# Storing one tile in thirteen pieces and waiting for the last stores in a section of their own

## The chip, the cores and the metric

The kernel runs on one core of one Trainium2 chip. The core has five engines that run side by side: TensorE (PE; its weight loads are shown apart as PEld), VectorE (DVE), ScalarE (ACT), GpSimd (POOL) and SyncE (SP), which here only issues DMA transfers and waits. Data moves between the chip's main memory and the on-chip memory (128 partitions) by 16 DMA engines. The metric is the device time of one execution in microseconds, as the median of several runs.

## The reference

```python
# x: (16, 512, 1024), weight: (1024, 768), bias: (768,), residual: (16, 512, 768), all float32
def reference(x, weight, bias, residual):
    return (np.matmul(x, weight) + bias + residual).astype(np.float32)
```

Seen as two dimensions, x has 8192 rows of 1024 numbers, and the output 8192 rows of 768.

## The kernel before

The 8192 rows are 64 tiles of 128 rows. Sixteen tiles (J, line 13) make one of four stretches S, and partition p holds the rows p*16 to p*16+15 of its stretch, so that a transfer of several tiles moves one long run per partition. A row of one tile in the output is 768 numbers, 3072 bytes.

For each tile, ScalarE (sometimes VectorE) casts the 128x1024 block of x to bf16 (`cast`, line 225), TensorE transposes it (`transp`, line 237), VectorE copies the transposed block out of PSUM, and TensorE multiplies it with the resident weight in sixteen matmuls (`mm_all`, line 264; each of eight weight halves, with 512 and 256 columns). GpSimd adds bias to residual (`pool_adds`, line 277), and VectorE adds the product to that (`finish`, line 291) in R, a ring of 32 tile rows that also receives the residual and is what is stored. The last tile, 63, is multiplied in two column parts of 512 and 256 (`LAST`, line 37), each added and stored by itself.

Nothing is issued as the program is written down. Every operation is recorded by `Program.add` (line 51) with what it reads and writes; `Program.emit` (line 62) then gives each engine its own list, and puts a wait on a semaphore before an operation only where no earlier wait already implies it (lines 89 to 105). A DMA gets a semaphore of its own (`landed_`, line 99), which has reached 16 when all parts of the transfer have landed.

All transfers go through SyncE, in the order of the list `ORDER` (lines 30 to 36). `pump` (line 165) takes the next entry when the recorded program has come far enough. An entry `('s', 3, 10, 11, 104)` stores, of stretch 3, the tiles from 10 to before 11 (tile 58 of all), cut at row 104: two transfers, of partitions 0 to 103 and 104 to 127 (lines 204 to 208). The stores at the end are: tiles 48 to 57 in one, tile 58 in two parts, tiles 59 and 60 in one, tile 61, tile 62, and the two column parts of tile 63 (`'c'`). SyncE waits for VectorE before each of them, so a store can be issued no earlier than the last add of its tiles, and no earlier than everything in front of it on SyncE.

Each store is given a name in `stores` (line 208), and a last operation on SyncE without an instruction of its own (line 362) depends on all of them: it only waits. `emit` leaves out those waits that others imply. The whole program stands in one section that the framework fences off (line 363): when SyncE's list is through, SyncE raises a semaphore; the other four engines, which wait for it, drain and report; SyncE collects the reports; and then all five go through the barrier that ends the program, in which GpSimd also clears the semaphores.

Of the kernel before, what the change touches and what calls it, by code (L numbers as in the profile page):

```python
# [14 lines left out]
RR = 32  # L15
# [16 lines left out]
 ('r', 0, 6, 16), ('x', 0, 14, 16), ('x', 1, 0, 6), ('r', 1, 0, 6), ('x', 1, 6, 16),  # L32
 ('r', 1, 6, 16), ('s', 0, 0, 16), ('x', 2, 0, 6), ('r', 2, 0, 6), ('x', 2, 6, 16),
 ('r', 2, 6, 16), ('s', 1, 0, 16), ('x', 3, 0, 6), ('r', 3, 0, 7), ('x', 3, 6, 16),
 ('r', 3, 7, 16), ('s', 2, 0, 16), ('s', 3, 0, 10), ('s', 3, 10, 11, 104), ('s', 3, 11, 13),
 ('s', 3, 13, 14), ('s', 3, 14, 15), ('c', 3, 15, 0), ('c', 3, 15, 1)]
LAST = [(0, 512), (512, 256)]


class Program:  # L40
# [10 lines left out]
    def add(self, eng, emit, rd=(), wr=(), dma=False):  # L51
        n, ops = len(self.ops), self.ops
        deps = {self.writer[k] for k in (*rd, *wr) if k in self.writer and (eng != "pe" or ops[self.writer[k]][0] != eng)}
        for k in wr:
            deps.update(d for d in self.readers.get(k, ()) if ops[d][0] != eng or ops[d][3])
        for k in rd:
            self.readers.setdefault(k, set()).add(n)
        for k in wr:
            self.writer[k], self.readers[k] = n, set()
        self.ops.append((eng, emit, deps - {n}, dma))  # L60

    def emit(self):
        ops, known = self.ops, {e: {} for e in self.engines}
        lane, count, snap, waits = [], {}, [], []
        for n, (eng, _, deps, dma) in enumerate(ops):
            mine = (n, 0) if dma else (eng, count.setdefault(eng, 0) + 1)
            if not dma:
                count[eng] += 1
            seen = known[eng]
            need = {}  # L70
            for d in deps:
                f, i = lane[d]
                if seen.get(f, -1) < i and i > need.get(f, (-1, 0))[0]:
                    need[f] = (i, d)
            need = {
                f: (i, d) for f, (i, d) in need.items()
                if not any(snap[d2].get(f, -1) >= i for g, (_, d2) in need.items() if g != f)
            }
            for f, (i, d) in need.items():
                for g, v in (*snap[d].items(), (f, i)):  # L80
                    if seen.get(g, -1) < v:
                        seen[g] = v
            waits.append([d for _, d in need.values()])
            lane.append(mine)
            own = dict(seen)
            own[mine[0]] = mine[1]
            snap.append(own)
        told = {d for w in waits for d in w}
        sems = {e: self.tc.alloc_semaphore(f"done_{e}") for e in self.engines if e != "sp"}
        total, mark = dict.fromkeys(self.engines, 0), {}  # L90
        for n, (eng, emit, _, dma) in enumerate(ops):
            e = self.engines[eng]
            for d in waits[n]:
                e.wait_ge(*mark[d])  # L94
            if emit is None:
                continue
            ins = emit(e)
            if dma:
                sem = self.tc.alloc_semaphore(f"landed_{n}")
                mark[n] = (sem, 16)  # L100
                ins.then_inc(sem, 16)
            elif n in told:
                total[eng] += 1
                mark[n] = (sems[eng], total[eng])
                ins.then_inc(sems[eng], 1)


@with_exitstack
def kernel(
# [8 lines left out]
    nc = tc.nc  # L118
# [33 lines left out]
    prog = Program(tc)  # L152
    op = prog.add

    def rows(a, b, cs=range(len(chunks))):
        return [("R", r % RR, c) for r in range(a, b) for c in cs]

    def dma(dst, src, rd, wr):
        op("sp", lambda e: e.dma_start(out=dst, in_=src), rd, wr, dma=True)  # L159
# [3 lines left out]
    stores = []  # L163

    def pump():
        while queue:
            kind, S, j0, j1, *cut = queue[0]
            if kind == "c":
                need = [("outc", j1)]
            elif kind in ("w", "b"):  # L170
                need = []
            elif kind == "x":
                need = [("cast", t - XR) for t in range(J * S + j0, J * S + j1) if t >= XR]
            elif kind == "r":
                need = [("store", t - RR) for t in range(J * S + j0, J * S + j1) if t >= RR]
                at = [t % RR for t in range(J * S + j0, J * S + j1)]
                if S < RR // J and any(W_ROW <= r < W_ROW + 2 * n_q for r in at):
                    need.append(("wcast", n_q - 1))
                if S < RR // J:
                    need += [("add", t) for t in range(EARLY_END) if TMP_ROW + t in at]  # L180
            else:
                need = [("out", J * S + j) for j in range(j0, j1)]
            if not all(n in done for n in need):
                return
            queue.pop(0)
            t0, nj = J * S + j0, j1 - j0
            if kind == "b":
                dma(bias_row.rearrange("(g p) n -> g p n", p=QUAD)[:, 0, :],
                    bias[None, :].to_broadcast([P // QUAD, N]), [], ["bias_row"])
                continue  # L190
            if kind == "w":
                dma(w_st[:, 2 * S + j0:2 * S + j1, :], w_d[:, S, j0:j1, :], [],
                    rows(W_ROW + 2 * S + j0, W_ROW + 2 * S + j1))
                continue
            if kind == "x":
                dma(X[:, t0 % XR:t0 % XR + nj, :], x_d[S, :, j0:j1, :], [],
                    [("X", t % XR) for t in range(t0, t0 + nj)])
            elif kind == "r":
                dma(R[:, t0 % RR:t0 % RR + nj, :], res_d[S, :, j0:j1, :], [], rows(t0, t0 + nj))
            else:  # L200
                n0, nl = (0, N) if kind == "s" else LAST[j1]
                cs = range(len(chunks)) if kind == "s" else [j1]
                j1 = j1 if kind == "s" else j0 + 1
                edges = [0, *cut, P]
                for p0, p1 in zip(edges, edges[1:]):
                    dma(out_d[S, p0:p1, j0:j1, n0:n0 + nl],
                        R[p0:p1, t0 % RR:t0 % RR + j1 - j0, n0:n0 + nl], rows(t0, t0 + j1 - j0, cs), [("out", len(stores))])
                    stores.append(("out", len(stores)))
                done.update(("store", J * S + j) for j in range(j0, j1))
            done.update((kind, J * S + j) for j in range(j0, j1))  # L210

    def mark(*what):
        done.add(what)
        pump()
# [31 lines left out]
    def times(po, lhsT, rhs, first, final, rd, wr):  # L246
        def emit(e):
            return e.add_instruction(mybir.InstMatmult(  # L248
                name=nc.get_next_instruction_name(),
                ins=[e.lower_ap(rhs), e.lower_ap(lhsT, for_matmul_weights=True)], outs=[e.lower_ap(po)],  # L250
                start_tensor_calc=first, stop_tensor_calc=final,
                tile_size=(P, P), tile_position=(0, 0), ldweights=False,
            ))
        op("pe", emit, rd, wr)
# [46 lines left out]
    def dummies(n, i):  # L301
# [10 lines left out]
        out=ident, in_=ident, compare_op=mybir.AluOpType.not_equal, fill=1.0, base=0,  # L312
        pattern=[[-1, P]], channel_multiplier=1,
    ), ["ident"], ["ident"])
    dummies(WARM, 0)

    pump()
    for kind, *a in HEAD_ORDER:
        if kind == "bias":
# [9 lines left out]
        elif kind == "wc":  # L329
            q, e, eng = a  # L330
            r = W_ROW + 2 * q + e
# [3 lines left out]
        else:  # L335
            mm_all(a[0], [a[1]])
    pump()
    for t in range(HEAD - 1):
        if ("fin", t) not in done:
# [11 lines left out]
    t = n_t - 1  # L351
    for i, (n0, nl) in enumerate(LAST):
        b = (t - 2 * i) % HEAD
# [5 lines left out]
    mark("out", t)  # L359
    pump()  # L360
    assert not queue, queue
    op("sp", None, stores)
    with tc.tile_critical():  # L363
        prog.emit()


# [28 lines left out]
```

## Time and profile before

| | us |
|---|---|
| median of 8 runs | 211.02 |
| lowest and highest of them | 210.71, 211.27 |
| the profiled execution, its own time | 211.61 |
| its span, first to last instruction | 209.83 |
| PE busy in the span | 200.3 (95%) |
| DVE, ACT, POOL busy | 105.4, 66.1, 115.1 |
| moved by DMA | 87.20 MB, mean 416 GB/s |

The page is one profiled execution. Its span leaves out 1.78 us of that execution's time. "SPq" in a view is SyncE's queue of DMA issues: a line gives the start and the duration of the issue, not of the transfer. Times in views count from the start of the span. The views leave out semaphore instructions, whose starts and durations the trace records too, as it does the start, size and duration of each packet (one row moved by one DMA engine) and the time of each landing.

### The profile page before, as it was taken

How to read it: one execution, taken by the hardware profiler on the slowest of the kernel's cores; microseconds unless marked ns; L12 is line 12 of the kernel's file. 1: busy time of each engine (PE TensorE's matmuls, PEld its weight loads, DVE VectorE, ACT ScalarE, POOL GpSimd, SP SyncE). 2: the span in 40 equal slices, each digit the busy share in tenths (PEclk: the TensorE clock that was granted, in tenths of full speed). 3: DMA queues.
4: the chain of work that ended last, by engine and by line, in shares of the span. 5: the costliest groups of instructions: out<-in, count | busy, mean ns of one | idle time of the engine just before them, and what ended most of it. 6: DMA issues, size and time to landing. Idle time of an engine off the chain costs nothing.

```text
span 209.8 us, 2462 instructions
## 1 busy us (share of the span) xinstructions
PE 200.3 (95%) x1273; PEld 80.8 (39%) x794; DVE 105.4 (50%) x141; ACT 66.1 (32%) x69; POOL 115.1 (55%) x71
## 2 busy tenths in 40 slices
PE   7899999999999999999999999999999999999990
PEld 2333433443444344334434443443344344434440
DVE  1457555445545554554455444645544554455460
ACT  2444513312730372310460083310280065230000
POOL 1100029769999805997039603999009931999000
PEclk9999999999999999999999999999999999999996
DMA  6999999999999898999999999998999999999993
GB/s 221 425 428 434 431 419 466 392 456 420 468 391 484 378 465 383 422 445 439 405 435 487 392 433 465 450 408 373 448 462 406 445 414 466 431 440 401 402 373 120
DMA packets 4924, 87.20 MB, mean 416 GB/s; under 512 B 557, under 2 KB 685, under 8 KB 1841
## 3 DMA queue, kind: packets, MB, share of 16 engines
q1 hardware_dynamic: 4913, 87.05, 97.4%
q8 instruction: 8, 0.13, 0.2%
q14 instruction: 3, 0.02, 0.0%
HBM read 61.88 MB, written 25.17 MB: 415 GB/s over the span
## 4 chain that ended last, share of the span: by engine, by line
PE 88%; DMA 7%; SPq 2%; issue 1%; ACT 0%; DVE 0%; ACTq 0%
PE psum_o L248 75%; PE pt L241 13%; DMA x_tile<-in_x_dram 7%; SPq L159 2%; ACT xb L217 0%; DVE ro L220 0%; SPq L390 0%; ACTq L94 0%; SPq L363 0%
## 5 line engine op out<-in xcount | busy, mean ns | idle before, releaser
L248 PE MATMUL psum_o<-w_sb,xt 128*128 128x256 bf16 (+1 forms) x999 | 175.3, 324 | 1.8 <-DVE xt L217 0.5
L220 POOL TENSOR_TENSOR ro<-ro,bias_sb 128x768 f32<-128x768 f32 x50 | 88.8, 1811 | 46.6 <-DMA ro<-in_residual_dram 46.6
L217 ACT CAST xb<-x_tile 128x1024 bf16<-128x1024 f32 (+1 forms) x63 | 61.3, 1022 | 117.2 <-DMA x_tile<-in_x_dram 75.7
L259 PEld LDWEIGHTS <-xt 128*128 128x128 bf16 x520 | 50.9, 98 | 102.9 <-issue 101.1
L217 DVE COPY xt<-pt 128x1024 bf16<-128x1024 bf16 x64 | 44.1, 691 | 84.4 <-PE pt L241 84.3
L220 DVE TENSOR_TENSOR ro<-psum_o,ro 128x768 f32<-128x768 f32 (+2 forms) x51 | 47.6, 934 | 5.4 <-POOL ro L220 3.3
L241 PE MATMUL pt<-ident,xb 128*128 128x128 f32 x256 | 38.3, 273 | 0.7 <-DVE xb L217 0.5
L220 POOL TENSOR_TENSOR ro<-ro 128x768 f32<-128x768 f32 x14 | 24.9, 1811 | 25.1 <-DMA ro<-in_residual_dram 24.9
L241 PEld LDWEIGHTS pt<-ident,xb 128*128 128x128 f32 x256 | 29.8, 141 | 15.7 <-issue 13.2
L220 DVE TENSOR_TENSOR ro<-psum_o,bias_sb 128x768 f32<-128x768 f32 x14 | 13.2, 948 | 0.0
L303 PE MATMUL psum_o<-warm 128*128 128x512 bf16 x18 | 6.3, 508 | 1.4 <-DVE warm_a L223 1.4
L217 DVE CAST xb<-x_tile 128x512 bf16<-128x512 f32 (+1 forms) x4 | 1.9, 492 | 6.2 <-DMA x_tile<-in_x_dram 6.2
L217 ACT CAST w_sb<-ro 128x768 bf16<-128x768 f32 x4 | 3.3, 832 | 3.8 <-DMA ro<-in_weight_dram 3.8
L217 POOL CAST w_sb<-ro 128x768 bf16<-128x768 f32 x1 | 0.8, 824 | 6.0 <-DMA ro<-in_weight_dram 6.0
L303 PEld LDWEIGHTS psum_o<-warm 128*128 128x128 bf16 x18 | 2.2, 125 | 4.5 <-issue 2.7
L217 DVE CAST w_sb<-ro 128x768 bf16<-128x768 f32 x3 | 1.7, 557 | 2.1 <-DMA ro<-in_weight_dram 2.1
L217 ACT ACT_TABLE_LOAD x1 | 1.3, 1283 | 0.9 <-SPq L363 0.9
L320 DVE STREAM_SHUFFLE bias_sb<-bias_row 128x768 f32<-128x768 f32 x1 | 1.0, 1007 | 0.0
L223 DVE MEMSET warm<- 128x256 uint32 x1 | 0.3, 272 | 1.1 <-SPq L363 1.1
L223 DVE MEMSET bias_row<- 128x768 f32 x1 | 0.7, 698 | 0.2 <-issue 0.2
L223 POOL MEMSET ident<- 128x128 f32 x1 | 0.2, 204 | 0.5 <-SPq L363 0.5
L311 POOL TENSOR_SCALAR_AFFINE_SELECT ident<-ident 128x128 f32<-128x128 f32 x1 | 0.3, 292 | 0.2 <-POOL ident L223 0.2
(7 smaller groups left out, 0.7 us busy)
## 6 DMA issues: line engine op xcount, KB each, us to landing
out_dram<-ro SPq DMA_DIRECT2D x3, 6144.0 KB, 34.1
x_tile<-in_x_dram SPq DMA_DIRECT2D x3, 5120.0 KB, 24.5
ro<-in_residual_dram SPq DMA_DIRECT2D x3, 3840.0 KB, 31.9
x_tile<-in_x_dram SPq DMA_DIRECT2D x3, 3072.0 KB, 39.5
ro<-in_residual_dram SPq DMA_DIRECT2D x3, 2304.0 KB, 18.6
x_tile<-in_x_dram SPq DMA_DIRECT2D x4, 1024.0 KB, 11.0
x_tile<-in_x_dram SPq DMA_DIRECT2D x2, 2048.0 KB, 23.5
out_dram<-ro SPq DMA_DIRECT2D x1, 3840.0 KB, 12.8
```

What stands on the lines that cost most here:

```text
L159: op("sp", lambda e: e.dma_start(out=dst, in_=src), rd, wr, dma=True)
L217: op(eng, lambda e: (e.copy if eng == "act" else e.tensor_copy)(out=dst, in_=src), rd, wr)
L220: op(eng, lambda e: e.tensor_add(out=dst, in0=a, in1=b), rd, wr)
L223: op(eng, lambda e: e.memset(dst, v), [], [wr])
L241: op("pe", lambda e, q=q: e.transpose(out=pt[:, q, :], in_=words[:, ts(q, P)], identity=ident), [("XB", t % XB_N, 2 * q // n_q), "ident"], ...
L248: return e.add_instruction(mybir.InstMatmult(name=nc.get_next_instruction_name(), ins=[e.lower_ap(rhs), e.lower_ap(lhsT, for_matmul_weight ...
L259: op("pe", lambda g: g.ldweights(lhsT), rd)
L303: op("pe", lambda e: e.matmul(PO[i][:, 0:512], lhsT=warm[:, 0:P], rhs=warm, start=True, stop=True), ["warm"], [("PO", i)])
L311: op("pool", lambda e: e.affine_select(out=ident, in_=ident, compare_op=mybir.AluOpType.not_equal, fill=1.0, base=0, pattern=[[-1, P]], ch ...
L320: op("dve", lambda e: e.stream_shuffle(out=bias_sb, in_=bias_row, mask=[0] * QUAD), ["bias_row"], ["bias"])
```

## The change

Two edits. Tile 58 is stored in thirteen transfers in place of two: partitions 0 to 47, 48 to 50, 51 to 62, then eleven, ten, nine and so on down to two partitions. And the waits for the stores are no longer an operation of the recorded program: `emit` returns the semaphores and values of all stores; SyncE waits for all but the last four of them (tiles 61 and 62 and the two parts of tile 63) at the end of the first section, and for those four in a second section in which SyncE alone takes part. The first section's exit, with all engines reporting to SyncE, so stands between the two groups of waits. These waits are written out one by one, without leaving out those that others imply: beside the thirteen pieces of tile 58, the stores of tiles 0 to 15, 16 to 31, 32 to 47, 48 to 57, and 59 with 60 are waited for in the first section.

```diff
- ('r', 3, 7, 16), ('s', 2, 0, 16), ('s', 3, 0, 10), ('s', 3, 10, 11, 104), ('s', 3, 11, 13),
+ ('r', 3, 7, 16), ('s', 2, 0, 16), ('s', 3, 0, 10), ('s', 3, 10, 11, 48, 51, 63, 74, 84, 93, 101, 108, 114, 119, 123, 126), ('s', 3, 11, 13),
  ('s', 3, 13, 14), ('s', 3, 14, 15), ('c', 3, 15, 0), ('c', 3, 15, 1)]
+OUTSIDE = 4
...
-    def emit(self):
+    def emit(self, ends):
...
-            if emit is None:
-                continue
             ins = emit(e)
...
+        return [mark[n] for n in ends]
...
                     dma(out_d[S, p0:p1, j0:j1, n0:n0 + nl],
-                        R[p0:p1, t0 % RR:t0 % RR + j1 - j0, n0:n0 + nl], rows(t0, t0 + j1 - j0, cs), [("out", len(stores))])
-                    stores.append(("out", len(stores)))
+                        R[p0:p1, t0 % RR:t0 % RR + j1 - j0, n0:n0 + nl], rows(t0, t0 + j1 - j0, cs), [])
+                    stores.append(len(prog.ops) - 1)
...
-    op("sp", None, stores)
     with tc.tile_critical():
-        prog.emit()
+        landed = prog.emit(stores)
+        for sem, value in landed[:-OUTSIDE]:
+            nc.sync.wait_ge(sem, value)
+    with tc.tile_critical(sync_engine=mybir.EngineType.SP):
+        for sem, value in reversed(landed[-OUTSIDE:]):
+            nc.sync.wait_ge(sem, value)
```

## The prediction

> **What bounds the kernel now.** I read the page's chain first, then the chain in order of time from 190 us on, to see where the work that sets the end stops being TensorE's.
>
> ```profile
> PE 88%; DMA 7%; SPq 2%; issue 1%; ACT 0%; DVE 0%; ACTq 0%
> ...
> 199.03 5.21 PE psum_o L248 x32
> 204.24 0.02 issue
> 204.27 0.42 DVE ro L220
> ```
>
> Up to 204.2 us the kernel is a TensorE kernel, and the change touches nothing there. The last add ends at 204.69. The span is 209.83, so 5.1 us come after all arithmetic: stores, their landings, and the way out of the program. Next I cut this stretch by time (columns: stretch, its length, busy time of PE, PEld, DVE, ACT, POOL, granted clock, share of the 16 DMA engines, GB/s).
>
> ```profile
> 201.00:205.00 4.00, 3.23 (x20) 1.67 (x17) 2.08 (x3) 0.00 (x0) 0.00 (x0) 1.00 0.95 377
> 205.00:206.00 1.00, 0.00 (x0) 0.00 (x0) 0.00 (x0) 0.00 (x0) 0.00 (x0) 1.00 0.85 332
> 206.00:207.00 1.00, 0.00 (x0) 0.00 (x0) 0.00 (x0) 0.00 (x0) 0.00 (x0) 0.84 0.49 175
> 207.00:208.00 1.00, 0.00 (x0) 0.00 (x0) 0.00 (x0) 0.00 (x0) 0.00 (x0) 0.50 0.05 18
> 208.00:210.00 2.00, 0.00 (x0) 0.00 (x0) 0.00 (x0) 0.00 (x0) 0.00 (x0) 0.50 0.00 0
> ```
>
> The reader is to see the row of 207 to 208: 0.05 of 16 engines is 0.8 of one engine. One DMA engine is still storing when fifteen are done. The trace's records of single packets and landings say the same: fifteen of the last store's sixteen parts land by 207.19, the sixteenth at 208.16, 0.97 us later; its data ends at 207.83, that of the others by 206.74. Then SyncE's waits go: the last landing's wait ends at 208.18, two more already fulfilled follow at 0.067 us each, and the program ends at 209.83. So 1.65 us lie behind the last landing.
>
> Third, SyncE's queue when it issues the stores of the end (start, duration; the first two are tile 58, rows 0 to 103 and 104 to 127, then tiles 59 and 60, 61, 62 and the two parts of 63).
>
> ```profile
> 191.54 0.35 SPq L159 DMA_DIRECT2D out_dram<-ro  x1
> 191.93 1.25 SPq L159 DMA_DIRECT2D out_dram<-ro  x1
> 197.61 0.35 SPq L159 DMA_DIRECT2D out_dram<-ro  x1
> 200.65 0.36 SPq L159 DMA_DIRECT2D out_dram<-ro  x1
> ...
> 204.72 0.90 SPq L159 DMA_DIRECT2D out_dram<-ro  x1
> ```
>
> Two are long: the second part of tile 58 (1.25) and the last store (0.90). The first byte of the last store moves at 206.12, 0.50 after its issue ends.
>
> [...] The trace agrees on k: the 104-row store leaves 13 engine landings and one record at 192.05, before any data; the 24-row store 12 and one early. [...] here the landing comes 0.34 us after the last packet (207.83 to 208.16), and the change leaves that alone. [...]
>
> **The change, part 1: tile 58 cut differently.** [...]
>
> Who can take rows? By the packets, the engines end the store before tile 58 (tiles 48 to 57) at 198.94, 199.13, 199.26, 199.28, 199.67, 199.89, 200.02, 200.43, 200.50, and seven between 200.66 and 200.97: a spread of 2.0 us. The records do not name an engine[...]. A 3072-byte row takes 0.121, started 0.118 apart. The late engine is one that ends at 200.86 and then needs 2.2 us for its ten rows, because eight of its packets take 0.12 to 0.43 instead of 0.121.
>
> I add up per engine: end of tiles 48 to 57, plus rows x 0.118, then eight packets each of the next five stores (0.231, 0.118, 0.118, 0.081, 0.0425 apart: 4.7 us), none before its data can start (0.5 after its issue). For the kernel before, with 1.0 of slow packets on the late engine, this gives 207.80 against 207.83 in the trace; without them 206.80. For the kernel after: 206.4 to 206.5 with no slow packets, 206.7 with half a microsecond of them and 207.2 with a whole one on an engine with eight rows. The data thus ends 0.6 to 1.4 earlier in this execution, and 0.3 to 0.4 earlier where slow packets do not occur at all (206.80 to 206.4). The last issue should also lose its 0.90: while it stands, the late engine has over thirty packets queued.
>
> **Part 2: eleven more issues.** A following issue takes 0.43 and a gap of 0.045, by the second of the two stores at 62.48 and 62.96. Thirteen from 191.54: 0.395 for the first, 12 x 0.48 = 5.76, so SyncE is free at 197.7; with one hold like that of 1.25 (0.8 more) 198.5, with a second of a microsecond 199.5. Tiles 59 and 60 are ready at 197.61, behind all this on SyncE, so their issue slips by 0 to 2 us. What is late next: their packets. Engines reach them only at about 199.6 (earliest, three rows after 199.26) to 201.5, and my sum is unmoved for an issue as late as 200; at 201 it gives 206.6, at 202 207.6. Cover gone, each further microsecond costs one. Tiles 61 and 62 are ready at 200.65 and 202.65, and nothing else is queued on SyncE; no engine waits for these rows of R.
>
> **Part 3: the landings.** Added on SyncE: waits for two old stores and eleven pieces, some ten instructions in the first section, 0.067 each when fulfilled: 0.67 after the last issue (205.1 to 205.6), so 206.3 at the latest. Then the exit of the first section, which before runs from 208.31 to 208.85 (0.54), at about 206.9, beside the last packets and landings: hidden. If cover were gone it would cost what it does today. After the last landing, before: two waits (0.13), branch to exit (0.16), drain (0.09), collecting five engines (0.21), two drains to the barrier (0.14). After: one branch, exit, drain, one NoOp, two drains; one wait (0.067) and most of the collection (0.211 to about 0.085) fall away: 0.067 + 0.126 = 0.19 saved. Bounds: 0 if the second section's own entry is late, 0.35 if its no-ops cost nothing. The final barrier and clearing (0.9) stay.
>
> **The sum.** The profiled execution took 211.61: span 209.83 and 1.78 around it. In it I expect 206.7 instead of 207.83 for data (-1.1) and -0.2 for the exit: 210.3. The median of the runs shown is 211.02, 0.6 less, so some slow packets may be of the profiled execution alone. With all of them the median goes to 209.7, with none (-0.4 - 0.2) to 210.4. I take 210.0.
>
> **The rivals.**
> 1. *Short stores are slow to issue* (slower). For it: the only two issues seen with k under 16 that follow another at once took 0.65 (bias) and 1.25 (24 rows), neither 0.43. Against it: the 104-row store also has k under 16 and took 0.35 after its wait, like 16-engine stores; two 16-engine loads were held for 1.60 and 1.34 at 95.6 and 144.1, while a 16 KB instruction fetch ran, so holds come without small k. It decides from about 0.86 per piece: then tiles 59 and 60 are issued at 202.2 and the data ends at today's 207.83. At 0.9 the end is 1.1 later than now: 211.02 + 1.1 - 0.2 = 211.9. At 1.25 they go at 207.4, data ends at 213.0, and the time is 216.
> 2. *The low engines are not the early ones.* Then 15 rows fall on an engine that ends at 200.97: +5 x 0.118 = 0.6 on such an engine, against the 1.0 of slow packets now: 210.8 to 211.4, no change.
> 3. *The cut does nothing, the section alone works*: slow packets follow whichever engine is last[...]. 211.02 - 0.2 = 210.8, inside what cannot be told. If the added waits end after the last landing, not even that: 211.0.
>
> **How the numbers follow.** The forecast has 0.60 (209.4 to 210.6), rivals 2 and 3 together 0.15, rival 1 with anything else that delays the last stores 0.25, of which half lies above 212.5. A measurement of this kernel tells from no change what exceeds about 0.2%, 0.42 us: faster is under 210.60, slower over 211.44. So 0.60 faster, 0.15 same, 0.25 slower. The range goes from 209.5 to 212.5, with under a tenth left out below and an eighth above; the forecast's own range is 209.4 to 210.6.
>
> **What would show it.** Right: the DMA share of the last stretch with data falls from many engines to none within half a microsecond, with no stretch of 0.05; the sixteen landings of the last store lie within 0.5; the thirteen issues end before 200; the last issue takes under 0.5; and the time from last landing to end is 1.45 instead of 1.65. Wrong: tiles 59 and 60 issued after 202, a DMA share well under 0.9 between 200 and 204, or again one engine behind the rest by a microsecond[...].

## The result and the profile after

The changed kernel takes 211.6 us in the median of 11 runs (211.30 to 211.78); the kernel before, run beside it, 210.89. The ratio is 1.0029, with a 95% interval of 1.0020 to 1.0039: slower by 0.6 us, which is small but clear of the noise. Faster by 1.0 had been forecast.

The chain and the chain in order of time show that TensorE's part is as it was:

```profile
PE 91%; DMA 4%; issue 1%; ACT 1%; DVE 1%; SPq 0%
...
198.96 5.21 PE psum_o L249 x32
204.17 0.02 issue
204.19 0.42 DVE ro L221
```

The difference lies after, and in SyncE's queue of issues (start, duration):

```profile
191.47 0.34 SPq L160 DMA_DIRECT2D out_dram<-ro  x1
191.85 1.10 SPq L160 DMA_DIRECT2D out_dram<-ro  x1
193.00 1.02 SPq L160 DMA_DIRECT2D out_dram<-ro  x1
...
196.54 1.21 SPq L160 DMA_DIRECT2D out_dram<-ro  x1
...
200.01 0.29 SPq L160 DMA_DIRECT2D out_dram<-ro  x1
...
201.64 0.36 SPq L160 DMA_DIRECT2D out_dram<-ro  x1
202.04 0.43 SPq L160 DMA_DIRECT2D out_dram<-ro  x1
...
204.75 1.11 SPq L160 DMA_DIRECT2D out_dram<-ro  x1
```

Of the twelve pieces that follow the first, six hold SyncE for 1.10, 1.02, 1.19, 1.21, 1.21 and 1.84, and the last six for 0.25 to 0.30. Tiles 59 and 60, finished at 197.5, are issued at 201.64 in place of 197.61. What that does to the DMA engines is seen in the stretches (length, busy time of PE, PEld, DVE, ACT, POOL, clock, DMA share, GB/s; a share near 1 means all sixteen engines busy). First the kernel before, then the changed one:

```profile
201.00:202.00 1.00, 1.00 (x7) 0.49 (x5) 0.33 (x1) 0.00 (x0) 0.00 (x0) 1.00 0.99 390
202.00:203.00 1.00, 1.00 (x7) 0.41 (x5) 0.62 (x1) 0.00 (x0) 0.00 (x0) 1.00 1.01 399
```

```profile
201.00:202.00 1.00, 1.00 (x7) 0.45 (x5) 0.41 (x1) 0.00 (x0) 0.00 (x0) 1.00 0.37 135
202.00:203.00 1.00, 1.00 (x6) 0.49 (x5) 0.55 (x1) 0.00 (x0) 0.00 (x0) 1.00 0.62 249
203.00:204.00 1.00, 1.00 (x10) 0.69 (x8) 0.61 (x1) 0.00 (x0) 0.00 (x0) 1.00 1.03 418
...
206.00:207.00 1.00, 0.00 (x0) 0.00 (x0) 0.00 (x0) 0.00 (x0) 0.00 (x0) 1.00 1.00 383
207.00:208.00 1.00, 0.00 (x0) 0.00 (x0) 0.00 (x0) 0.00 (x0) 0.00 (x0) 1.00 0.44 152
208.00:210.00 2.00, 0.00 (x0) 0.00 (x0) 0.00 (x0) 0.00 (x0) 0.00 (x0) 0.85 0.01 4
```

The shares of 0.99 and 1.01 between 201 and 203 have become 0.37 and 0.62: the engines run dry. The last packet of tile 58 ends at 202.34, and the first sixteen packets of tiles 59 and 60 start between 202.48 and 202.63. From 203 to 207 the shares are 0.94 to 1.03, and all stop together: the last store's sixteen landings lie between 207.75 and 207.91. No engine is late in this execution. That all of them had waited for the same store is a likely reason, but it isn't shown; with padding, below, the same cut has a late engine again. The last landing is 0.25 earlier than in the profiled execution before, and yet the span is no shorter, because the way out grew. From the trace's semaphore instructions and landings, in us:

```
                          last landing   to the end of the span   outside the span
before                        208.16             1.67                   1.78
changed                       207.91             2.00                   1.78
```

In the changed kernel SyncE pauses on its way out, between two of its drains at 208.34 and 208.80, which before stood 0.06 apart; the next fetch of 8 KB of instructions comes at 209.44, where the kernel before has none.

### The profile page after: what moved, and what is told of

It reads as the page before. It is cut to its first block, busy times and chain, and to the rows that moved or that the text cites. A ratio compares the mean times of both kernels' runs of the same rounds, so it can differ in the third digit from the quotient of the medians.

```text
span 209.9 us, 2488 instructions
## 1 busy us (share of the span) xinstructions
PE 199.9 (95%) x1273; PEld 80.8 (38%) x794; DVE 105.4 (50%) x141; ACT 66.1 (32%) x69; POOL 115.1 (55%) x71
## 4 chain that ended last, share of the span: by engine, by line
PE 91%; DMA 4%; issue 1%; ACT 1%; DVE 1%; SPq 0%
PE psum_o L249 78%; PE pt L242 13%; DMA x_tile<-in_x_dram 4%; ACT xb L218 1%; SPq L160 0%; DVE xt L218 0%; DVE ro L221 0%; SPq L395 0%; SPq L363 0%
```

## The experiments

**The two edits apart.** The cut alone is the kernel before with the list entry of the thirteen pieces; the section alone is the changed kernel with the old entry.

```diff
 # the cut alone
-('s', 3, 10, 11, 104)
+('s', 3, 10, 11, 48, 51, 63, 74, 84, 93, 101, 108, 114, 119, 123, 126)
 # the section alone: the reverse, in the changed kernel
```

> The kernel before with the thirteen pieces alone; the landings are waited for as before. Theory A (the short stores hold SyncE about 1.1 us each, so tiles 59 and 60 are issued at about 201.6 in place of 197.6 and the DMA engines run dry between 202 and 204; the cut carries the loss on the data side, the second section carries a loss of its own at the exit): issue of tiles 59 and 60 at 201.3 to 202, last landing near 207.9, last landing to end about 1.7, time 0.1 to 0.4 us above the kernel before, and 0.2 to 0.4 below the changed kernel. Theory B (the second section costs everything, the cut nothing): time equal to the kernel before within 0.1.

> The changed kernel with tile 58 in two pieces of 104 and 24 rows as before; only the second section is new. Theory A: issues as in the kernel before; from last landing to end 1.45 if the pause of 0.46 us in SyncE's way out comes with the longer list of SyncE in the changed kernel (time 0.1 to 0.2 below before), 1.9 to 2.0 if it belongs to the second section itself (time 0.2 to 0.4 above before). Theory B: all of the loss, 0.6 us above before.

The cut alone: 211.72, ratio 1.0034 (1.0020 to 1.0048). Seven issues of 0.47 to 1.39, tiles 59 and 60 at 201.35, the same dry stretch, last landing 207.63. The section alone: 210.62, ratio 0.9986 (0.9978 to 0.9995), and from last landing to end 1.40. So the cut carries the loss and the section is a gain; two expectations failed: the cut alone is not 0.2 to 0.4 below the changed kernel, and it is 0.7 above the kernel before, not 0.1 to 0.4. Part of the reason lies outside the span. In the run with the cut alone the way out inside the span took 1.92, against 1.67 before, with three more fulfilled waits behind the last landing and more semaphores to clear (by estimate 0.26: three times the 0.067 of a fulfilled wait before, and 352 ns of clearing in place of 288); and 2.15 lie outside, against 1.78 before. An extra of about 0.4 appears in both kernels with the thirteen pieces, once before the end of the span and once behind it.

The stretches of the section alone also show that the late engine, which I had read from the row of 207 to 208 with a share of 0.05 in the kernel before, does not come with every execution of this cut:

```profile
205.00:206.00 1.00, 0.00 (x0) 0.00 (x0) 0.00 (x0) 0.00 (x0) 0.00 (x0) 1.00 0.98 376
206.00:207.00 1.00, 0.00 (x0) 0.00 (x0) 0.00 (x0) 0.00 (x0) 0.00 (x0) 0.82 0.39 137
207.00:208.00 1.00, 0.00 (x0) 0.00 (x0) 0.00 (x0) 0.00 (x0) 0.00 (x0) 0.50 0.00 0
```

Tile 58 is cut at row 104 here too, and no engine is late: the last landing is at 207.19.

**Is it the few engines?** Rival 1 blamed stores on fewer than sixteen engines; its k is the number of engines on which a transfer lands. In the changed kernel the pieces of 3, 12, 11 and so on to 2 rows leave as many landings as they have rows, each besides one record before its data (193.11 for the piece issued at 191.85), and the first piece, of 48 rows, leaves sixteen. By estimate from these counts a piece of sixteen rows runs on sixteen engines, with one row on each.

```diff
-('s', 3, 10, 11, 104)
+('s', 3, 10, 11, 16, 32, 48, 64, 80, 96, 112)
```

> The kernel before with tile 58 in eight pieces of sixteen rows[...]; waits as before. If only stores on fewer than sixteen engines are held: the seven following issues take about 0.43 each, tiles 59 and 60 are issued at 197.6, time within 0.3 of before. If every store issued behind another while long packets (30720 bytes, 1.14 us) are in flight is held for about one such packet: seven of about 1.15, tiles 59 and 60 at about 200, time up to 0.2 above before.

SyncE's issues in that run:

```profile
191.38 0.34 SPq L159 DMA_DIRECT2D out_dram<-ro  x1
191.77 1.19 SPq L159 DMA_DIRECT2D out_dram<-ro  x1
...
195.50 1.21 SPq L159 DMA_DIRECT2D out_dram<-ro  x1
196.75 1.12 SPq L159 DMA_DIRECT2D out_dram<-ro  x1
197.92 1.10 SPq L159 DMA_DIRECT2D out_dram<-ro  x1
199.06 0.42 SPq L159 DMA_DIRECT2D out_dram<-ro  x1
199.52 0.42 SPq L159 DMA_DIRECT2D out_dram<-ro  x1
```

Six holds of 1.10 to 1.22 with pieces of sixteen rows. And in the changed kernel the last store, with sixteen landings, took 1.11 at 204.75, while the six pieces with seven to two landings took 0.25 to 0.30. Few engines are not the cause. Tiles 59 and 60, issued at 199.52, 1.9 later than before, cost nothing: 210.84, ratio 0.9993 (0.9983 to 1.0003). Slack of about two microseconds is what the prediction had worked out for this store, and it is there.

**Four pieces with the same slope.** The pieces have 32, 44, 27 and 25 rows. That they load the engines with a slope like that of the thirteen is the author's estimate; no landing names its engine.

```diff
-('s', 3, 10, 11, 104)
+('s', 3, 10, 11, 32, 76, 103)
```

> The kernel before with tile 58 in four pieces of 32, 44, 27 and 25 rows[...], a slope like that of the thirteen; waits as before. Theory A: three held issues of about 1.2, done by 195.7, tiles 59 and 60 at 197.6 as before, DMA share stays above 0.9 from 201 to 205, landing by 207.2, time 0 to 0.6 below before. If the slope itself is what hurts: last landing at 208 or later, time above before.

The three following pieces took 1.56, 1.23 and 1.06, and tiles 59 and 60 went at 197.62. The time is that of the kernel before, 1.0003 (0.9993 to 1.0013); the last store's landings still spread from 206.42 to 207.40, against 206.40 to 207.19 in the run with the section alone, which has two pieces. Cutting with this slope in mind brought nothing here.

**Does a hold last as long as a packet in flight?** The holds of 1.1 to 1.2 looked like the 1.14 of the packets of 30720 bytes that the engines were storing. Two runs shorten those packets.

```diff
 # beside the cut: packets of 15360 bytes
-('s', 3, 0, 10)
+('s', 3, 0, 5), ('s', 3, 5, 10)
 # of 6144 bytes
+('s', 3, 0, 2), ('s', 3, 2, 4), ('s', 3, 4, 6), ('s', 3, 6, 8), ('s', 3, 8, 10)
```

> The run with the cut alone, but tiles 48 to 57 are stored in two transfers of five tiles, so that the packets in flight while the thirteen pieces are issued are of 15360 bytes (about 0.57 us) in place of 30720 (1.14). If a hold lasts for one packet in flight: holds of 0.55 to 0.65, thirteen pieces done by about 198.5, tiles 59 and 60 issued by 199, time 0.5 or more below the cut alone and about that of the kernel before. If the hold has a length of its own: 1.0 to 1.2 again, tiles 59 and 60 at 201.3, time as the cut alone.

> The cut alone, with tiles 48 to 57 stored in five transfers of two tiles, so that from 192.3 us on the packets in flight are of 6144 bytes (0.23 us). In the run with packets of 15360 bytes the holds were 1.02 to 1.1. If a hold lasts for a number of bytes or packets in flight: holds clearly under 0.8 from 192.5 on. If it has a length of its own: 1.0 to 1.1 again, up to about 199.

With 15360 bytes:

```profile
191.99 1.10 SPq L159 DMA_DIRECT2D out_dram<-ro  x1
...
195.32 1.08 SPq L159 DMA_DIRECT2D out_dram<-ro  x1
196.44 1.07 SPq L159 DMA_DIRECT2D out_dram<-ro  x1
```

With 6144 bytes:

```profile
195.23 1.08 SPq L159 DMA_DIRECT2D out_dram<-ro  x1
196.35 1.07 SPq L159 DMA_DIRECT2D out_dram<-ro  x1
197.47 1.74 SPq L159 DMA_DIRECT2D out_dram<-ro  x1
```

The guess falls: most holds are 1.0 to 1.1 with packets of 0.23 and 0.57 us and 1.0 to 1.2 with packets of 1.14; single ones are longer, up to 1.84. The first of these two kernels takes 211.63 (1.0025, 1.0016 to 1.0034); the second was run once with a profile, 211.52. In the runs so far with eight or thirteen pieces the short issues begin between 199.0 and 199.7, at or soon after the time when the first engine ends the store of tiles 48 to 57 and moves a packet of the pieces (198.9 to 199.2). What SyncE waits for while the pieces queue up stays open.

**Is it the late store of tiles 59 and 60?** Here the pieces stand behind that store.

```diff
-..., ('s', 3, 10, 11, 48, ..., 126), ('s', 3, 11, 13), ...
+..., ('s', 3, 11, 13), ('s', 3, 10, 11, 48, ..., 126), ...
```

> The run with the cut alone, but the thirteen pieces stand behind the store of tiles 59 and 60 in the order, so this store is issued at 197.6 as in the kernel before; waits as before. If the late issue of tiles 59 and 60 is what the cut costs: no dry stretch between 202 and 204, and a time 0.2 to 0.6 below the cut alone, though tile 61 may now be issued at 203 in place of 200.65. If the pieces themselves (small, on few engines) are what costs: time as the cut alone, 211.6 or more.

The hoped-for time did not come: 213.08, ratio 1.0087 (1.0061 to 1.0113; four runs). The stretches show why:

```profile
203.00:204.00 1.00, 1.00 (x10) 0.76 (x8) 0.54 (x1) 0.00 (x0) 0.00 (x0) 1.00 0.42 132
204.00:205.00 1.00, 0.23 (x3) 0.00 (x0) 0.58 (x2) 0.00 (x0) 0.00 (x0) 1.00 0.13 43
205.00:206.00 1.00, 0.00 (x0) 0.00 (x0) 0.00 (x0) 0.00 (x0) 0.00 (x0) 1.00 0.54 203
206.00:207.00 1.00, 0.00 (x0) 0.00 (x0) 0.00 (x0) 0.00 (x0) 0.00 (x0) 1.00 1.02 406
```

Tiles 59 and 60 went at 197.61, but now tile 61, ready near 200.6, stood behind thirteen issues and went at 204.65. The dry stretch moved to 203 to 205.5 and became longer, the last landing to 209.03. It was not the expected proof for tiles 59 and 60, and by its time alone the run fits the other branch of the expectation too. The issue time of tile 61 and the place of the dry stretch decide: what is queued on SyncE behind the pieces runs late, and the engines run dry. A run that only delays one store, without the pieces, was not made.

This run also says more of the holds:

```profile
198.69 1.08 SPq L159 DMA_DIRECT2D out_dram<-ro  x1
...
200.74 0.79 SPq L159 DMA_DIRECT2D out_dram<-ro  x1
201.57 0.34 SPq L159 DMA_DIRECT2D out_dram<-ro  x1
```

Three of the pieces are held here, for 1.08, 0.88 and 0.79, and the short issues begin at 201.57. The engines reach the pieces later too: the first packet of a piece moves at 200.75. So a hold has no fixed length (0.79 to 1.84 in these runs), and the holds end neither at a fixed time nor after a fixed number of pieces, but soon after the engines reach the pieces (the short issues begin at 201.57 after 200.75 here, at 199.67 after 199.01 in the changed kernel). That is not the whole of it: in the changed kernel two later stores are long too, 0.85 at 202.58 and 1.11 at 204.75.

**The pause.** Sixty instructions with fulfilled waits on SyncE at 158 us lengthen its list where it has nothing to do; first with the section alone, then in the changed kernel. Sixty is an estimate: 120 waits, two to an instruction, as eight instructions from 205.97 to 206.41 hold them in the trace of the changed kernel.

```diff
+            if dma and n == self.pad_after:      # the store of tiles 32 to 47
+                for _ in range(120):
+                    e.wait_ge(*mark[waits[n][0]])
```

> The kernel with the second section alone (tile 58 in two pieces), and sixty more instructions on SyncE that wait for something already fulfilled, after the store of tiles 32 to 47 at about 158 us, where SyncE is idle for 30 us. Nothing else differs from the run with the section alone (210.62, exit 1.40 after the last landing). If the 0.46 us pause at the exit of the changed kernel, and the 0.37 us outside the span of the run with the cut alone, come from the length of SyncE's list (one more 8 KB fetch of instructions near the end): about 0.4 us above the section alone, and a fetch near or after the end. If they come from the number of transfers or semaphores: no difference.

> The changed kernel with the sixty fulfilled waits of the padded run put on SyncE at about 158 us. If the pause of 0.46 us in SyncE's way out belongs to the place in SyncE's list where a further 8 KB of instructions is fetched, the fetch at 209.4 moves to about 165 and the pause goes: last landing to end 1.5 in place of 2.0, time about 0.4 below the changed kernel (211.2), unless the fetch at 165 makes one DMA engine late as in the padded run. If the pause belongs to the thirteen transfers or their semaphores: it stays, time 211.6.

In both, the fourth 8 KB fetch now comes at 165 us (165.1 and 165.7), where the section alone had none and the changed kernel had it at 209.44. In the changed kernel the pause is gone: from last landing to end 1.49 in place of 2.00, as expected. So in the changed kernel the pause went when a longer list of SyncE moved the fetch from 209.44 to 165.7; the thirteen pieces and their waits had made the list longer before. How the fetch would bring the pause about is not shown. The median is 211.42 (1.0020, 1.0011 to 1.0028), 0.2 below the changed kernel and not 0.4; and as the intervals of the two ratios overlap, even a gain in time is not shown. With the section alone, padding costs 0.48: 211.10, though its way out stays 1.41. An extra of 0.4 had been expected there, with a fetch near the end; the extra came, but the fetch came at 165, so the reason given was wrong. In its profile one engine lands the last store 0.76 behind the fifteenth, and in the profile of the padded changed kernel, at 212.01 the slowest of its runs, 0.80. That the fetch at 165 makes this engine late is likely from the two, but not shown.

**No cut at all.** Tile 58 in one transfer, with the section and without it.

```diff
-('s', 3, 10, 11, 104)
+('s', 3, 10, 11)
```

> The second section, and tile 58 stored in one transfer of 128 rows. If the cut at row 104 is worth something in the kernel before: slower than the section alone by 0.2 or more, with seven or so engines landing the last store 0.3 to 0.8 after the others. If the spread of engines is absorbed by the time between issues: equal to the section alone (210.6) within 0.1, so below both kernels.

> The kernel before with tile 58 stored in one transfer of 128 rows, waits as before. With the second section the uncut store gave 210.34 against 210.62 for the two pieces. If cut and section are independent: 0.25 to 0.35 below the kernel before, with its exit of 1.65. If the gain of the uncut store needs the section: equal to the kernel before.

With the section 210.34, ratio 0.9967 (0.9953 to 0.9980): below both kernels, and the fastest here. Without it 210.65, 0.9976 (0.9968 to 0.9984). Both came out lower than expected: 0.3 below the section alone, where equal or slower had been the two branches, and 0.5 below the kernel before in place of 0.25 to 0.35. Within the intervals the gain of the section and that of the uncut store add. The way out is 1.40 with the section and 1.67 without: the section is worth 0.27 on the path. The stretches with the section, uncut:

```profile
204.00:205.00 1.00, 0.20 (x2) 0.00 (x0) 0.55 (x2) 0.00 (x0) 0.00 (x0) 1.00 0.84 335
205.00:206.00 1.00, 0.00 (x0) 0.00 (x0) 0.00 (x0) 0.00 (x0) 0.00 (x0) 1.00 1.00 382
206.00:207.00 1.00, 0.00 (x0) 0.00 (x0) 0.00 (x0) 0.00 (x0) 0.00 (x0) 1.00 0.27 94
207.00:208.00 1.00, 0.00 (x0) 0.00 (x0) 0.00 (x0) 0.00 (x0) 0.00 (x0) 1.00 0.00 0
```

The uncut kernels are the best ones to set the cut against, as their profiles have no late engine. In profiled executions, without the section, the cut into thirteen takes 211.70 and the uncut store 210.64: the last landing is 0.43 later, the way out 0.26 longer, and 0.37 more lies outside the span. With the section it is 211.69 against 210.28: the last landing is 0.82 later and the way out 0.60 longer. So the late stores are about half of the loss, and the end of the program is the rest. The eight pieces land no later than the uncut store (207.12 against 207.19); they lose 0.22 on the way out.

**The kernel before, traced again.**

> The kernel before once more, for a second trace. If the engine that stored 0.97 us behind the others at the end was an event of the one execution: the sixteen landings of the last store lie within 0.8 us and the last landing is near 207.2. If it belongs to the kernel: again one landing about 1 us behind the fifteenth.

Two engines are late this time: the last landing (208.31) is 0.39 behind the fifteenth, which is itself 0.58 behind the fourteenth. This execution took 211.77. Both profiles of the kernel before thus have late engines, and both lie near the top of its runs (210.5 to 211.8). The section alone, with the same cut, had none in its profile; nor had the two uncut kernels, whose last two landings lie 0.17 and 0.10 apart. Why two pieces at times leave an engine late stays open.

## Why the prediction was wrong

- **Part 2, the price of an issue: the step that failed.** "A following issue takes 0.43" was read from an issue at 62.96 that the prediction called a store; it is a load of x behind a store. The pieces, issued before the engines had reached them, took 1.0 to 1.2 and once 1.84, six of twelve in all. The 1.25 of the 24-row store was the right row, and I had booked it as a single accident. Thirteen issues ended at 201.59, not between 197.7 and 199.5, and tiles 59 and 60 went at 201.64.
- **The sum, term by term.** For the profiled execution 210.3 was forecast and 211.69 measured, 1.4 more. The prediction's own figures for a late issue (data end at 206.6 for 201, at 207.6 for 202) give 207.2 for 201.64 in place of 206.7: 0.5 of it. The data in fact ended at 207.56, by the packets: another 0.4. From the first packet of tiles 59 and 60 to the last of all, five stores took 5.08, where the sum has 4.7; what made them slower is not shown. The way out was to be 0.2 shorter and was 0.33 longer: the last 0.5. So the right price of an issue would have brought the forecast near no change (by the same working, from 0.8 faster to 0.2 slower); that the kernel became slower lies in the other two terms.
- **Rival 1** named the right place, and nearly the size: the mean over the twelve following pieces is 0.82 with the gap (191.85 to 201.64), just under its break-even of 0.86. (That 0.86 includes the gap between issues; its 0.9 and 1.25 leave it out.) Its cause, few engines, is wrong, and its break-even came too late: an issue of tiles 59 and 60 at 202.2 was set against the late engine's end. Against a last landing of 207.2 it lies between 199.5 (no loss with sixteens) and 201.4 (loss with the cut alone).
- **Part 1, what there was to win.** The 1.0 us of the late engine was read from one execution near the top of the range, though the prediction did allow that some of it might belong to that execution alone. Uncut and unbalanced, the last store lands at 207.1 to 207.2. The sum for the kernel after gave each engine its own number of rows. The landings show how many engines a piece ran on (16, then 3, 12, 11 and so on to 2) and not which, so these shares, and with them rival 2's low engines, were the author's estimate. It found no support: a cut into four pieces, meant to have a like slope, left the time where it was (1.0003). One sign of being right came true by luck, the sixteen landings within 0.5 (0.17): nothing shows the engines balanced; they had run dry before, with shares of 0.37 and 0.62. The last issue, which was to take under 0.5, took 1.11.
- **Part 3, the landings.** The saving was right and larger than said: 0.27 for 0.19. The waits were hidden as said (the first section's exit ends at about 207.0). Left out were the pause of SyncE, 0.40 more between the two drains and 0.11 in the second of them, and GpSimd's clearing of eleven more semaphores, 352 in place of 288 ns. So the change as a whole lengthens the way out by 0.33.

## What to carry to other kernels

Price a row of issues by one from the same stretch and with the same work in flight, as the 1.25 at 191.93 was, and not by any transfer that follows another: in the changed kernel a store behind a store took 1.10 at 191.85, 0.29 at 200.01 and 0.43 at 202.04. Then ask for each store behind them when its data was ready. One late engine in one profile is no budget: look whether the execution is typical of the runs before planning to win it back. Here a single transfer of all 128 rows came out faster than two, four, eight and thirteen pieces, and taking the common exit off the path of the last landings was worth 0.3 us by itself.

## What the runs showed of the hardware that was not expected

- Stores of tile 58's pieces issued in a row held SyncE for 1.0 to 1.2 us each in most cases (0.8 to 1.8 at the extremes) from the second one on, with pieces of sixteen rows as with pieces that left 3 to 12 landings, and with packets of 6144 to 30720 bytes in flight. They took 0.25 to 0.47 soon after the first engine had moved a packet of the pieces: packet and first short issue came at 199.01 and 199.67 in the changed kernel, at 198.93 and 199.06 with eight pieces, and at 200.75 and 201.57 with the pieces behind tiles 59 and 60. The reason is open.
- SyncE paused at the program's end: in the changed kernel 0.46 between two drains, and in its padded form, where the fourth 8 KB fetch came at 165.7 in place of 209.44, 0.06. In the other four kernels with thirteen pieces and no padding this fetch came after the end of the span. Three of them have it 1.9 us behind the end, and 2.09 to 2.18 outside the span in place of 1.78 to 1.82; the fourth, with packets of 6144 bytes, has it 0.3 behind the end, and neither a pause nor extra time. So the fetch alone does not decide, and whether the time outside the span comes from it is not shown.
- Clearing the semaphores at the end took GpSimd 288 ns before, 352 with eleven more transfers and 373 with fifteen more.
